# Token parts of 256 and 288 instead of 272 and 272 in the projections, and a 64 byte tile beside h

## The chip, the core and the metric

The kernel runs on one core of one Trainium2 chip. The metric is device time in microseconds (us) for one launch; lower is better. TensorE is PE in the profile, its weight loads are PEld, VectorE is DVE, ScalarE is ACT, GpSimd is POOL, SyncE is SP, and SP issues the DMA transfers.

## What is computed

One inference step of a one-layer decoder. There are 512 prompt tokens and 32 sample tokens (8 requests of 4), 544 in all, of width 1024. The reference, cut to what the change touches:

```python
shift, scale, gate = split(silu(c) @ w_cond + b_cond, 3)
h = x * (1 + scale[:, None]) + shift[:, None]
[qa, ka, va, za, qkv_b, zb, a_b, b_b, g_a, g_b] = h @ w_in      # 1024 -> 11280
ya = o_a * silu(za)                       # o_a: dilated attention, three head groups
yb = rms_norm(o_b) * silu(zb)             # o_b: gated delta rule after a short convolution
merged = sigmoid(g_a) * (ya @ w_branch_a) + sigmoid(g_b) * (yb @ w_branch_b)
y = layer_norm(ALPHA * x + gate[:, None] * (merged @ w_out)) * ln_g + ln_b
```

It also returns the new key and value caches, convolution states and delta-rule states.

## The kernel before

**Projections.** Features lie on the partitions, tokens along the free dimension. A weight of 128 output columns arrives as a tile `wt` of 128 x 1024 float32 (8 blocks of 128 x 128, one for each 128 input features). `split` makes of it `hi` (ACT, rounded to float32r) and `lo` (DVE, the rest). The activations are kept in the same two pieces, `hhi` and `hlo` (h), `ybh` and `ybl` (branch B), `yah` and `yal` (branch A), `x1h` and `x1l` (the first tiles). Each 128 x 128 block needs three products: `hi` with the high part of h, `hi` with its low part, `lo` with the high part. In the profile these stand as `pp<-hhi,hi`, `pp<-hlo,hi` and `pp<-hhi,lo`: output, moving operand, weights. All are float32r.

**Two parts.** One PSUM tile (`pp`, 2 buffers) holds at most 512 float32 in a partition, so the 544 tokens are taken in two parts of `HF` = 272. `stream` runs a job's 24 products (8 blocks x 3) for part 0, hands the sum to the job's `evac`, and does the same for part 1. Each product loads its weights anew. There are 85 tiles of `w_in` in this loop, 8 of `w_branch_b`, and 8 of `w_branch_a` with 4 blocks instead of 8. The first three tiles of `w_in` are done ahead of it, from `x1h` and `x1l` with sums in `pp`, `pd` and `pg`. The `evac` functions (`conv_job`, `attention_job`, `za_job`, `zb_job`, `gate_job`, `branch_job`) know where a part ends: the prompt's last 240 tokens and the 32 sample tokens are in part 1.

**The last stage.** `product_out` multiplies `mhi` and `mlo` (weights) with `wo0h`, `wo0l` (first 512 output columns) and `wo1h`, `wo1l` (the other 512) in products of 512 columns, and in two products of 256 for the last 128 tokens. It doesn't use `HF`.

**Addresses.** The pools `wsp` (two buffers each of `hi` and `lo`) and `hpool` (`hhi`, `hlo`) are allocated one after the other from the right end of SBUF, and the pool of `ybh` and `yal` behind them. One token row of h takes 544 x 4 = 2176 = 17 x 128 bytes, a part of 272 takes 1088 = 8 x 128 + 64. In the built program `hi` and `lo` begin at 96 modulo 128 in every buffer and block. `hhi` and `hlo` also begin at 96, so part 0 begins 0 bytes from the weights modulo 128, part 1 begins 64 bytes from them (`ybh` and `yal` likewise; `x1h`, `x1l`, `ybl` and `yah` begin at 32, so that it is the other way round there). `mhi` and `mlo` lie at 32 modulo 128, `wo0h` and `wo0l` at 32 (0 bytes apart), `wo1h` at 96 (64 bytes apart).

**Order.** The program is first recorded, then put in order by a list scheduler (`schedule`) that keeps a cost for each instruction (a float32r product's grows with its columns) and emits the instructions in its order of start, so that each engine's queue is fixed at build time. Attention, the delta rule and the sample tokens' work are put between the projection's products. SP issues all transfers in that order: weights, cache rows for the sample tokens, and the copies of old cache rows to the outputs (`out_kv_s<-in_cache`), which are spread over the span. All engine instructions are emitted by one line of `emit`, L727, so rows are told apart by tile names.

Of the kernel before, what the change touches and what calls it, by code (L numbers as in the profile page):

```python
# [23 lines left out]
NTD = 4  # L24
NS = NB * NTD
NT = SEQ + NS
HF = NT // 2
PROJ = 11280
OFF_Q, OFF_K, OFF_V, OFF_ZA, OFF_B, OFF_ZB, OFF_AB, OFF_GA, OFF_GB = (
    0, 1536, 3072, 4608, 5120, 8192, 9216, 9232, 10256)  # L30
# [219 lines left out]
class Recorder:  # L250
# [21 lines left out]
    def pool(self, make, name, bufs, side):  # L272
        return Pool(self, make, name, bufs, side)
# [506 lines left out]
def body(ctx, tc, io):  # L780
# [11 lines left out]
    keep = pool(ctx, "keep", 1)  # L792
    wsp = pool(ctx, "wsp", 2, "right")
    hctx = ExitStack()
    hpool = pool(hctx, "hpool", 1, "right")
    psp = bank("psp", BANKS[0])
    psd = bank("psd", BANKS[1])
# [13 lines left out]
    def pp():  # L811
        return psp.tile([128, 512], F32, name="pp", tag="pp")
# [79 lines left out]
    abT = op.tile([128, NT], F32, name="abT", tag="o")[0:32]  # L892
    xs = xT[:, :, SEQ:].rearrange("p k (b t) -> p k b t", t=4)
    per_token = lambda t, k, n: t[:, k:k + n, 1:9, None].to_broadcast([128, n, 8, 4])
    cols_of = lambda n: slice(n * HF, (n + 1) * HF)
    with ExitStack() as fctx:
        fr = pool(fctx, "front", 1)
        cT = fr.tile([128, KT, 9], F32, name="cT")
# [59 lines left out]
            return pv[:, :, 0:9], bT[:, 8 * part + at:8 * part + at + m, None].to_broadcast([128, m, 9])  # L958

        x1 = [fr.tile([128, KT, NT], F32R, name=f"x1{u}") for u in "hl"]  # L960
        sums = [[f()[:, :HF] for _ in range(2)] for f in (pp, pd, pg)]
        for b, (c, m) in enumerate(CHUNKS):
            pv, bias = cond_block(1, c, m, b % 2)
            kk = slice(c, c + m)
# [26 lines left out]
        for n in range(2):  # L991
            for k in range(KT):
                for x in range(2):
                    pe.matmul(ps[n][0:32, :HF], hl[:, k], x1[x][:, k, cols_of(n)],
                              start=(k == 0 and x == 0), stop=(k == KT - 1 and x == 1))
        for n in range(2):
            se.activation(abT[:, cols_of(n)], ps[n][0:32, :HF], AF.Copy)
        for c, m in two_by_two:
            pv, bias = cond_block(0, c, m, c % 4)
            kk = slice(c, c + m)  # L1000
# [42 lines left out]
    def stream(until):  # L1043

        while done[0] < until:
            i = done[0]
            job = jobs[i]
            for x in range(i, min(i + 5, len(jobs))):
                if x not in raws:
                    raws[x] = wraw.tile([128, D], F32, name="wt", tag="wraw")  # L1050
                    jobs[x].load(raws[x])
                if x <= i + 1 and x not in weights:
                    weights[x] = split(raws[x], jobs[x].nk * 128, ve)
            if job.start:
                yield job.start
            if job.begin:
                job.begin()
            (hi, lo), (xhi, xlo) = weights.pop(i), job.x
            for n in range(2):
                ps = pp()[:, :HF]  # L1060
                cols = slice(n * HF, (n + 1) * HF)
                for k in range(job.nk):
                    a, b = hi[:, k * 128:(k + 1) * 128], lo[:, k * 128:(k + 1) * 128]
                    for w, x in ((a, xhi), (a, xlo), (b, xhi)):
                        pe.matmul(ps, w, x(k)[:, cols], start=(k == 0 and w is a and x is xhi),
                                  stop=(k == job.nk - 1 and w is b))
                    if k < job.nk - 1:
                        yield 0
                job.evac(n, ps)
                if n and job.after:  # L1070
                    job.after()
                if not n:
                    yield 0
            done[0] += 1
            threads.set(job.over, 0.0)
            yield 0
# [4 lines left out]
    def column_job(name, **kw):  # L1081
        return Job(name[0], lambda raw: sp.dma_start(raw, io["w_in"][TILE_AT[name]]), KT, of_h, **kw)

    half = lambda t, n: t[:, n * HF:(n + 1) * HF]


    moves = [(g, b, r, min(r + MOVE, w - 4)) for g, (w, _) in enumerate(GROUPS) for b in range(8) for r in range(0, w - 4, MOVE)]
# [133 lines left out]
    def conv_job(h, s):  # L1221
# [19 lines left out]
        def evac(n, ps):  # L1241
            if not n:
                head_of_ext()
                se.activation(t["ext"][:, 3:275], ps, AF.Copy)
                return
            ext = t["ext"]
            es = ext[:, 515:571].rearrange("p (b w) -> p b w", w=7)
            se.activation(ext[:, 275:515], ps[:, 0:240], AF.Copy)
            se.activation(es[:, :, 3:7], ps[:, 240:272].rearrange("p (b t) -> p b t", t=4), AF.Copy)
            convolve()  # L1250

        def shifted(raw, by):
# [290 lines left out]
    def attention_job(j, g, s):  # L1543

        def begin():
            pairs[j][s, g] = spare()[:, :SEQ] if s == 2 else ap.tile([128, 512], F32, name="qk"[s], bufs=3)

        def evac(n, ps):
            t, scale = pairs[j][s, g], 1.0 if s else -0.125
            if g == 0:  # L1550
                lo, hi = ((0, 272), (272, 512))[n]
                se.activation(t[:, lo:hi], ps[:, 0:hi - lo], AF.Copy, scale=scale)
            else:
                v = t.rearrange("p (r a n) -> p n a r", r=4, a=4)
                m = (17, 15)[n]
                se.activation(v[:, 17 * n:17 * n + m], ps[:, 0:16 * m].rearrange("p (n a r) -> p n a r", a=4, r=4),
                              AF.Copy, scale=scale)
            if n:
                se.activation((qs, ks, vs)[s][:, j, g if s else at_g(g), :], ps[:, 240:272], AF.Copy, scale=scale)
                if s == 2:  # L1560
                    threads.set(ready[j, g], 2.5)

        return column_job(("a", j, g, s), evac=evac, begin=begin, start=(freed[j - 1] if j else began,))
# [954 lines left out]
```

## Time and profile before

| | |
|---|---|
| median of 3 runs | 886.1 us (883.63 to 886.37) |
| profiled execution, span | 886.1 us |
| TensorE clock granted, mean | 0.995 |
| PE | 864.7 us, 8176 instructions |
| DVE, ACT, POOL | 643.4, 451.7, 68.7 us |
| DMA | 236.18 MB, queue q1 79.0% of 16 engines' span |

[...] Products overlap, so the time that one costs in a run of products is the distance from one start to the next, here called the interval. It is read from the timeline's starts or from a long run in the chain of waits, divided by the count.

### The profile page before, as it was taken

Reading aid. Unit: us, or ns where it says so; the run is one execution under the profiler, and the core shown is the slowest. Engines: PE = TensorE matmul, PEld = TensorE weight load, DVE = VectorE, ACT = ScalarE, POOL = GpSimd, SP = SyncE. Lnnn points to the kernel's source line nnn. Section 1 sums busy time; section 2 is a strip of 40 time slices with the busy share of each in tenths; the row PEclk is TensorE's granted clock in tenths of the full one; section 3 lists DMA queues with packets and bytes.
Section 4 is the critical chain, followed back from the end, with each engine's and each line's share of the span. In section 5 each row is a group of like instructions: output and inputs, shape, how many; then the busy total and the mean of one; then the engine's idle time right before and its main releaser. Section 6 shows DMA issues by size and latency. Waiting matters only on the chain.

```text
span 886.1 us, 20733 instructions
## 1 busy us (share of the span) xinstructions
PE 864.7 (98%) x8176; PEld 818.1 (92%) x8176; DVE 643.4 (73%) x1330; ACT 451.7 (51%) x1073; POOL 68.7 (8%) x167
## 2 busy tenths in 40 slices
PE   8999999999999999999999999999999999999994
PEld 7889999898999899999999988999899999999884
DVE  4675557564458899968999753556899699998547
ACT  3546656765546696347775446732442222324324
POOL 0120110110001110002120000021010000001000
PEclk9999999999999999999999999999999999999998
DMA  9876768666687886889877885479869899987973
GB/s 334 337 212 199 234 219 268 235 206 214 198 256 249 282 278 207 271 265 329 303 227 257 262 291 186 169 219 293 330 223 375 275 402 420 377 285 235 348 248 142
DMA packets 121069, 236.18 MB, mean 267 GB/s; under 512 B 49174, under 2 KB 76640, under 8 KB 118284
## 3 DMA queue, kind: packets, MB, share of 16 engines
q1 hardware_dynamic: 120972, 234.86, 79.0%
q8 instruction: 64, 1.05, 0.5%
q14 instruction: 33, 0.27, 0.1%
HBM read 218.53 MB, written 103.97 MB: 364 GB/s over the span
## 4 chain that ended last, share of the span: by engine, by line
PE 82%; DMA 6%; DVE 5%; ACT 5%; issue 1%; SPq 1%; POOL 0%; DVEq 0%; ACTq 0%
PE pp L727 62%; PE pg L727 9%; PE pd L727 7%; PE pb L727 4%; DMA wc<-in_w_cb 2%; ACT L727 1%; DVE r L727 1%; DMA slab<-in_ks 1%; DMA dO<-orow 1%; DMA S<-in_state_delta 1%; DMA wv<-dw 1%; ACT hi L727 1%; DMA out_kv_s<-in_cache 1%; SPq L727 1%; ACT sq L727 1%
## 5 line engine op out<-in xcount | busy, mean ns | idle before, releaser
L727 PE MATMUL pp<-hhi,hi 128*128 128x272 f32 x1360 | 400.2, 294 | 1.7 <-DVE zt L727 1.0
L727 PE MATMUL pp<-hhi,lo 128*128 128x272 f32 x1360 | 401.3, 295 | 0.0
L727 PE MATMUL pp<-hlo,hi 128*128 128x272 f32 x1360 | 398.1, 293 | 0.0
L727 PEld LDWEIGHTS pp<-hhi,hi 128*128 128x128 f32 x1360 | 257.0, 189 | 4.6 <-issue 1.8
L727 PEld LDWEIGHTS pp<-hhi,lo 128*128 128x128 f32 x1360 | 256.7, 189 | 2.1 <-issue 1.4
L727 PEld LDWEIGHTS pp<-hlo,hi 128*128 128x128 f32 x1360 | 257.1, 189 | 1.5 <-issue 0.4
L727 ACT ACTIVATE hi<-wt 128x1024 fp32r<-128x1024 f32 (+1 forms) x101 | 103.6, 1026 | 171.2 <-PE pp L727 130.1
L727 DVE TENSOR_TENSOR lo<-wt,hi 128x1024 fp32r<-128x1024 f32 (+1 forms) x101 | 119.0, 1178 | 74.9 <-ACT hi L727 74.4
L727 DVE SCALAR_TENSOR_TENSOR acc<-ext,cw,acc 128x568 f32<-128x568 f32 x72 | 58.0, 805 | 1.6 <-ACT acc L727 0.6
L727 DVE TENSOR_TENSOR slab<-slab 128x512 f32<-128x512 f32 (+1 forms) x66 | 43.1, 669 | 6.7 <-DMA slab<-in_ks 4.5
L727 DVE TENSOR_REDUCE slab<-slab 128x8 f32<-128x512 f32 (+2 forms) x66 | 42.7, 660 | 3.3 <-ACT slab L727 3.0
L727 ACT ACT_TABLE_LOAD x32 | 41.1, 1283 | 4.1 <-DMA dO<-orow 1.6
L727 ACT ACTIVATE zt<-pp 128x272 f32<-128x272 f32 x48 | 18.7, 390 | 38.7 <-PE pp L727 37.3
L727 PE MATMUL pp<-ybh,lo 128*128 128x272 f32 x128 | 36.9, 288 | 0.0
L727 PE MATMUL pp<-ybh,hi 128*128 128x272 f32 x128 | 36.9, 288 | 0.0
L727 PE MATMUL pp<-ybl,hi 128*128 128x272 f32 x128 | 36.9, 288 | 0.0
L727 ACT ACTIVATE P<-P,st 128x256 f32<-128x256 f32 (+1 forms) x64 | 31.1, 488 | 11.2 <-DVE st L727 11.1
L727 POOL COPY cx<-ext 128x3 f32<-128x3 f32 (+1 forms) x48 | 21.7, 480 | 151.0 <-ACT ext L727 149.5
L727 DVE CUSTOM_DVE_ANT_0 P<-pg,bias 128x256 f32<-128x256 f32 (+1 forms) x64 | 23.0, 403 | 13.8 <-PE pg L727 13.7
L727 ACT ACTIVATE spare<-pp 128x272 f32<-128x272 f32 (+1 forms) x32 | 16.2, 506 | 16.1 <-PE pp L727 16.1
L727 PEld LDWEIGHTS pp<-ybh,hi 128*128 128x128 f32 x128 | 24.1, 189 | 0.2
L727 PEld LDWEIGHTS pp<-ybh,lo 128*128 128x128 f32 x128 | 24.2, 189 | 0.1
(421 smaller groups left out, 1548.8 us busy)
## 6 DMA issues: line engine op xcount, KB each, us to landing
out_kv_s<-in_cache SPq DMA_DIRECT2D x144, 512.0 KB
wt<-in_w_in SPq DMA_DIRECT2D x85, 512.0 KB
out_kv_s<-in_cache SPq DMA_DIRECT2D x24, 496.0 KB
wc<-in_w_cb SPq DMA_DIRECT2D x16, 512.0 KB
slab<-in_ks SPq DMA_DIRECT2D x32, 256.0 KB
slab<-in_vs SPq DMA_DIRECT2D x32, 256.0 KB
kv<-in_ks SPq DMA_DIRECT2D x16, 512.0 KB
kv<-in_vs SPq DMA_DIRECT2D x16, 512.0 KB
```

Source lines behind the costliest of these rows:

```text
L727: getattr(real[x.engine], x.name)(*map(arg, x.args), **{k: arg(v) for k, v in x.kw.items()})
```

## The change

Every projection takes its tokens as 256 and 288 instead of 272 and 272: `HF` goes, `HALVES` and `WIDTH` come, and each `evac` uses the new bounds (256 prompt tokens in part 0; 256 prompt and 32 sample tokens in part 1). A pool `apart` with one tile `gap` of 16 float32 (64 bytes) is opened between `wsp` and `hpool`, and GpSimd clears it once. In the built program `hi` and `lo` stay at 96 modulo 128, and `hhi`, `hlo`, `ybh` and `yal` are at 32; `x1h`, `x1l`, `ybl` and `yah` stay at 32. 256 columns take 1024 = 8 x 128 bytes, so both parts now begin 64 bytes from the weights modulo 128.

```diff
-HF = NT // 2
+HALVES = (slice(0, 256), slice(256, NT))
+WIDTH = (256, NT - 256)
...
     hctx = ExitStack()
+    apart = pool(hctx, "apart", 1, "right")
+    gap = apart.tile([128, 16], F32, name="gap")
+    ge.memset(gap, 0.0)
     hpool = pool(hctx, "hpool", 1, "right")
...
-    cols_of = lambda n: slice(n * HF, (n + 1) * HF)
+    cols_of = lambda n: HALVES[n]
...
-        sums = [[f()[:, :HF] for _ in range(2)] for f in (pp, pd, pg)]
+        sums = [[f()[:, :w] for w in WIDTH] for f in (pp, pd, pg)]
...
             for n in range(2):
-                ps = pp()[:, :HF]
-                cols = slice(n * HF, (n + 1) * HF)
+                ps, cols = pp()[:, :WIDTH[n]], HALVES[n]
...
-                se.activation(t["ext"][:, 3:275], ps, AF.Copy)
+                se.activation(t["ext"][:, 3:259], ps, AF.Copy)
...
-            se.activation(ext[:, 275:515], ps[:, 0:240], AF.Copy)
-            se.activation(es[:, :, 3:7], ps[:, 240:272].rearrange("p (b t) -> p b t", t=4), AF.Copy)
+            se.activation(ext[:, 259:515], ps[:, 0:256], AF.Copy)
+            se.activation(es[:, :, 3:7], ps[:, 256:288].rearrange("p (b t) -> p b t", t=4), AF.Copy)
...
-                m = (17, 15)[n]
-                se.activation(v[:, 17 * n:17 * n + m], ps[:, 0:16 * m].rearrange("p (n a r) -> p n a r", a=4, r=4),
+                se.activation(v[:, 16 * n:16 * n + 16], ps[:, 0:256].rearrange("p (n a r) -> p n a r", a=4, r=4),
                               AF.Copy, scale=scale)
```

The scheduler's costs change with the columns, so a few instructions change places. On PE, in the first tiles of attention, the transposes of the value tile (`pg<-cst,spare`) and of a delta-rule head (`pb<-cst,KQ`) stand between a projection's products. Before:

```order
L727 MATMUL pp<-hlo,hi 128x272
L727 MATMUL pp<-hhi,lo 128x272
L727 MATMUL pg<-cst,spare 128x128 x2
L727 MATMUL pp<-hhi,hi 128x272
L727 MATMUL pp<-hlo,hi 128x272
L727 MATMUL pp<-hhi,lo 128x272
L727 MATMUL pp<-hhi,hi 128x272
L727 MATMUL pp<-hlo,hi 128x272
L727 MATMUL pb<-cst,KQ 128x128 x4
L727 MATMUL pp<-hhi,lo 128x272
```

Now, on the same engine at the same place:

```order
L728 MATMUL pp<-hhi,lo 128x288
L728 MATMUL pp<-hhi,hi 128x288
L728 MATMUL pg<-cst,spare 128x128 x2
L728 MATMUL pp<-hlo,hi 128x288
L728 MATMUL pp<-hhi,lo 128x288
L728 MATMUL pp<-hhi,hi 128x288
L728 MATMUL pp<-hlo,hi 128x288
L728 MATMUL pp<-hhi,lo 128x288
L728 MATMUL pb<-cst,KQ 128x128 x4
L728 MATMUL pp<-hhi,hi 128x288
```

Five products stand between the two groups as before; each group stands one product further on. Of the 4800 float32r projection products with 128 output features, 4535 were followed directly by another before, and 4528 are now.

On SP, in the middle of the program, the cached keys of the sample tokens (`slab`), a weight tile (`wt`) and the copies of cache rows are issued in turn. Before:

```order
L727 DMA slab<-in_ks 128x512
L727 DMA wt<-in_w_in 128x1024
L727 DMA slab<-in_ks 128x512
L727 DMA out_kv_s<-in_cache 16x8192
L727 DMA slab<-in_ks 128x512 x2
L727 DMA out_kv_s<-in_cache 16x8192
L727 DMA slab<-in_ks 128x512 x2
```

Now, on SP at the same place:

```order
L728 DMA slab<-in_ks 128x512 x2
L728 DMA wt<-in_w_in 128x1024
L728 DMA out_kv_s<-in_cache 16x8192
L728 DMA slab<-in_ks 128x512 x2
L728 DMA out_kv_s<-in_cache 16x8192
L728 DMA slab<-in_ks 128x512 x2
```

One more piece of the cached keys now stands ahead of the weight tile; the copies keep their places between the others.

More of the change, by code (lines that the diff above doesn't have):

```diff
@@ L993, in body @@
                 for x in range(2):
-                    pe.matmul(ps[n][0:32, :HF], hl[:, k], x1[x][:, k, cols_of(n)],
+                    pe.matmul(ps[n][0:32, :WIDTH[n]], hl[:, k], x1[x][:, k, cols_of(n)],
                               start=(k == 0 and x == 0), stop=(k == KT - 1 and x == 1))
         for n in range(2):
-            se.activation(abT[:, cols_of(n)], ps[n][0:32, :HF], AF.Copy)
+            se.activation(abT[:, cols_of(n)], ps[n][0:32, :WIDTH[n]], AF.Copy)
         for c, m in two_by_two:
@@ L1082, in column_job @@
         return Job(name[0], lambda raw: sp.dma_start(raw, io["w_in"][TILE_AT[name]]), KT, of_h, **kw)
-    half = lambda t, n: t[:, n * HF:(n + 1) * HF]
+    half = lambda t, n: t[:, HALVES[n]]
     moves = [(g, b, r, min(r + MOVE, w - 4)) for g, (w, _) in enumerate(GROUPS) for b in range(8) for r in range(0, w - 4, MOVE)]
@@ L1550, in evac @@
             if g == 0:
-                lo, hi = ((0, 272), (272, 512))[n]
-                se.activation(t[:, lo:hi], ps[:, 0:hi - lo], AF.Copy, scale=scale)
+                se.activation(t[:, 256 * n:256 * n + 256], ps[:, 0:256], AF.Copy, scale=scale)
             else:
                 v = t.rearrange("p (r a n) -> p n a r", r=4, a=4)
-                m = (17, 15)[n]
-                se.activation(v[:, 17 * n:17 * n + m], ps[:, 0:16 * m].rearrange("p (n a r) -> p n a r", a=4, r=4),
+                se.activation(v[:, 16 * n:16 * n + 16], ps[:, 0:256].rearrange("p (n a r) -> p n a r", a=4, r=4),
                               AF.Copy, scale=scale)
             if n:
-                se.activation((qs, ks, vs)[s][:, j, g if s else at_g(g), :], ps[:, 240:272], AF.Copy, scale=scale)
+                se.activation((qs, ks, vs)[s][:, j, g if s else at_g(g), :], ps[:, 256:288], AF.Copy, scale=scale)
                 if s == 2:
```

## The prediction

> **What bounds the kernel now.** I read the page first, then the chain of waits, then the stages, then single intervals in the timeline of TensorE.
>
> ```profile
> span 886.1 us, 20733 instructions
> PE 864.7 (98%) x8176; PEld 818.1 (92%) x8176; DVE 643.4 (73%) x1330; ACT 451.7 (51%) x1073; POOL 68.7 (8%) x167
> ...
> PE 82%; DMA 6%; DVE 5%; ACT 5%; issue 1%; SPq 1%; POOL 0%; DVEq 0%; ACTq 0%
> ...
> L727 PE MATMUL pp<-hhi,hi 128*128 128x272 f32 x1360 | 400.2, 294 | 1.7 <-DVE zt L727 1.0
> L727 PE MATMUL pp<-hhi,lo 128*128 128x272 f32 x1360 | 401.3, 295 | 0.0
> L727 PE MATMUL pp<-hlo,hi 128*128 128x272 f32 x1360 | 398.1, 293 | 0.0
> ```
>
> The profiled span equals the median of the runs, 886.1 us, so the sum below is made against it with nothing added. TensorE is occupied for 98% and its largest group waits 1.7 us in all. Its stream of products sets the end; what one product costs in that stream is the question. The 294 ns of the page is not that cost, since products overlap. The chain gives it in long unbroken runs (start, length, count):
>
> ```profile
> 375.18 18.12 PE pp L727 x144
> 690.73 47.05 PE pp L727 x374
> ```
>
> 18.12/144 = 125.8 ns and 47.05/374 = 125.8 ns for one product of 272 columns. The granted clock is 1.00 in the windows below, so no throttle explains the number. Now the two parts apart. In h's job, 24 products make a part; the rows are first products of three parts in turn, the first part with its operands 64 bytes apart modulo 128 (tokens 272 to 543), the next 0 bytes apart:
>
> ```profile
> 376.28 0.29 PE L727 MATMUL pp<-hhi,hi 128*128 128x272 f32 x1
> ...
> 379.28 0.29 PE L727 MATMUL pp<-hhi,hi 128*128 128x272 f32 x1
> ...
> 382.32 0.29 PE L727 MATMUL pp<-hhi,hi 128*128 128x272 f32 x1
> ```
>
> 3.00/24 = 125.0 ns at 64 bytes, 3.04/24 = 126.7 ns at 0 bytes. **The distance alone is worth under 2 ns at 272 columns.** The last stage holds the other cases: `wo0h` lies 0 bytes from its weights, `wo1h` 64. The products of 256 columns, first and last row of 30 and of 48, and between them products of 512 at 64 bytes:
>
> ```profile
> 844.82 0.28 PE L727 MATMUL pp<-wo0h,mhi 128*128 128x256 f32 x1
> ...
> 848.27 0.28 PE L727 MATMUL pp<-wo0h,mlo 128*128 128x256 f32 x1
> ...
> 866.79 0.40 PE L727 MATMUL pp<-wo1l,mhi 128*128 128x512 f32 x1
> ...
> 869.35 0.28 PE L727 MATMUL pp<-wo1h,mhi 128*128 128x256 f32 x1
> ...
> 874.68 0.28 PE L727 MATMUL pp<-wo1h,mlo 128*128 128x256 f32 x1
> ```
>
> 256 columns at 0 bytes: 3.45/29 = 119.0 ns. 256 at 64 bytes: 5.33/47 = 113.4 ns. 512 at 64 bytes: 2.56/11 = 232.7 ns. Is the 113.4 only a quieter machine? The windows of these two stretches, and of the three parts of 272 above, say no (columns: length, then PE, PEld, DVE, ACT, POOL busy with counts, clock, DMA share, GB/s):
>
> ```profile
> 869.35:874.68 5.33, 5.33 (x48) 5.32 (x47) 5.14 (x11) 3.57 (x7) 0.00 (x0) 1.00 0.26 98
> 844.82:848.27 3.45, 3.45 (x31) 3.45 (x30) 0.42 (x1) 0.04 (x1) 0.00 (x0) 1.00 0.57 179
> 376.28:388.36 12.08, 12.08 (x99) 12.08 (x97) 10.80 (x31) 4.49 (x8) 0.00 (x0) 1.00 0.87 249
> ```
>
> The fast stretch is the one in which VectorE is full and ScalarE at two thirds; in the slow one both are nearly idle. The DMA was busier in the slow one, 0.57 against 0.26, but the run of 374 products kept its 125.8 ns beside a DMA share of 1.01 (the window from 700 us, below) as the other did at 0.87. I take it that address distance and length together set the interval.
>
> **The change part by part.** Products: 3 x 1360 of h, 3 x 128 of `ybh` and `ybl`, 3 x 64 of `yah` and `yal`, 9 groups of 16 of the first tiles: 4080 + 384 + 192 + 144 = 4800, in 2400 pairs of parts. Rows for the smaller groups:
>
> ```profile
> L727 PE MATMUL pp<-ybh,hi 128*128 128x272 f32 x128 | 36.9, 288 | 0.0
> ...
> L727 PE MATMUL pp<-yah,hi 128*128 128x272 f32 x64 | 18.5, 291 | 0.2 <-ACT yah L727 0.2
> ...
> L727 PE MATMUL pp<-x1l,hi 128*128 128x272 f32 x16 | 4.9, 313 | 0.0
> ```
>
> A pair costs 125.0 + 126.7 = 251.7 ns now. None is removed and none added; 16 columns move from one part to the other.
>
> *The part of 256.* Its nearest row has the same columns and the same distance: 113.4 ns. Bounds: 113.4 and 119.0 (the row at 0 bytes). I take 113.4, since in that stretch the interval was steady from the first product behind one of 512, and the weights there (`mhi`, `mlo`) came from 16 different tiles, so that no more than the distance modulo 128 was held fixed.
>
> *The part of 288.* No row shows 288. From below, 113.4 x 288/256 = 127.6 ns, if it runs at the good rate. From above, 126.7 x 288/272 = 134.2 ns. Two rows at the right distance, 64 bytes, stand on either side: 272 columns gave 125.0, which scales to 132.4; and on the line from 272 (125.0) to 512 (232.7), 16 columns more give 132.2. Both sides of 288 were slow at 64 bytes, although 512 columns, like 288, are a whole number of 128 bytes. So I take 132.3 ns: the second part gets nothing but its columns.
>
> *Sum.* 113.4 + 132.3 = 245.7 ns, 6.0 ns less for a pair. By the order of TensorE, 4535 of the 4800 products are followed directly by another; where a product of another kind stands behind, the columns cancel between the parts and I count nothing. 2267 pairs x 6.0 ns = 13.6 us.
>
> *What may not follow.* Two stages run near another limit:
>
> ```profile
> 340.00:380.00 40.00, 39.79 (x312) 39.07 (x311) 36.01 (x83) 19.65 (x50) 0.25 (x2) 1.00 0.78 245
> ...
> 700.00:760.00 60.00, 60.00 (x529) 59.07 (x529) 53.57 (x59) 16.61 (x29) 0.00 (x0) 1.00 1.01 402
> ```
>
> VectorE at 90% still has room for a TensorE that is 2.4% faster. The DMA engines are full from 700 to 760 us; if they hold the weights back there, 60 x 6.0/251.7 = 1.4 us is not gained. I count half, 0.7 us. In the order of SP one piece of the cached keys now stands ahead of a weight tile:
>
> ```profile
> slab<-in_ks SPq DMA_DIRECT2D x32, 256.0 KB
> ...
> L727 POOL COPY cx<-ext 128x3 f32<-128x3 f32 (+1 forms) x48 | 21.7, 480 | 151.0 <-ACT ext L727 149.5
> ```
>
> 256 KB at the 245 GB/s of the window from 340 us is some 1 us, hidden by the weight tiles loaded ahead: there are three `wt` buffers, each worth 24 x 251.7 ns = 6.0 us of products.
>
> *The small edits.* ScalarE's copies out of PSUM have the same total of columns. GpSimd's clear of `gap` is one small instruction at the start, on an engine that is busy 8%; if it were not covered it would cost some 0.5 us, as the copy of three columns does (480 ns, the row above). The first part is shorter, so its PSUM buffer must be emptied within 132.3 x 24 = 3.2 us instead of 3.0, the second within 2.7; the groups wait 1.7 us in all now, and I count nothing.
>
> 886.1 - 13.6 + 0.7 = 873.2, rounded to **873 us**.
>
> [...]
>
> **The rivals.** About 0.3% (2.7 us) is what a measurement here can tell from no change.
>
> 1. *Both parts run at the good rate.* For it: both are whole multiples of 128 bytes long and 64 apart, as in the steady stretch. Against it: 512 columns at 64 bytes, also a whole multiple, took 232.7, above 2 x 113.4 = 226.8. Pair 113.4 + 127.6 = 241.0: 10.7 x 2267 = 24.3 us, 862 us.
>
> 2. *The distance does nothing in the loop; only columns count.* For it: under 2 ns at 272. In the loop the moving tiles step by 2176 bytes and not by 2048 as `wo1h` does, and products of another kind come between. Pair 119.0 + 132.3 = 251.3: 0.4 x 2267 = 0.9 us, 885 us. The case that the change doesn't do what it says, since a distance fixed at build time makes no steady pattern in the loop, is this one.
>
> 3. *The part of 288 locks to the bad side: slower.* A steady pattern can be steadily bad. In a run of 272 some intervals are longer:
>
> ```profile
> 375.76 0.30 PE L727 MATMUL pp<-hhi,lo 128*128 128x272 f32 x1
> 375.90 0.29 PE L727 MATMUL pp<-hhi,hi 128*128 128x272 f32 x1
> 376.03 0.28 PE L727 MATMUL pp<-hlo,hi 128*128 128x272 f32 x1
> ```
>
> 0.27/2 = 135 ns. If every product of the second part were like that, plus 16 columns at 125.8/272 = 0.46 ns, it would be 142.4 ns, the pair 255.8, and 4.1 x 2267 = 9.3 us are lost: 895 us. It decides from 251.7 - 113.4 = 138.3 ns on. Against it: at 64 bytes both longer lengths have means near the others.
>
> **How the numbers follow.** The chances: forecast 0.50, both good 0.20, nothing 0.17, slower 0.13. The forecast's own range: 288 columns between 512's rate (232.7 x 288/512 = 130.9 ns) and that of the mixed runs (125.8 x 288/272 = 133.2), so 7.4 to 5.1 ns for a pair, 16.8 to 11.6 us, with 0 to 1.4 us lost to the DMA and 2 us either way for waits that change place: 868 to 878 us. The range for 8 in 10 reaches to both neighbours, 860 to 888 us. Faster by over 0.3%: the first two cases less a little for lost waits, 0.68; within 0.3%: 0.18, nearly all of it rival 2; slower: 0.14.
>
> **What would show it.** The rows of `128x256` and `128x288` in the profile after, and their intervals in long runs: 113.4 and 132.3 ns are forecast; 127.6 for the second is rival 1, 119 for the first rival 2, above 138.3 for the second rival 3. TensorE's waits should stay within a few us, and the rows of the last stage should keep their intervals. The forecast is wrong if the first part isn't steady at 113 in the loop, or if the stage from 700 to 760 us keeps its length.

## The result and the profile after

The median went from 884.32 us (882.89 to 886.53, 7 runs) to **890.22 us** (887.29 to 893.27, 7 runs). The ratio is 1.0057 with a 95% interval of 1.0035 to 1.0080: slower, by about 5 us. The forecast was 873, and the range of 860 to 888 does not hold it. (Further down, one run of `e10_order_268`, 940.54 us at a granted clock of 0.848, is left out of its median and ratio.) The profiled execution has a span of 888.5 us, against 886.1 before. The page after, in the rows that answer to those shown of before (span, engines, shares of the chain of waits, largest group):

```profile
span 888.5 us, 20739 instructions
PE 862.7 (97%) x8176; PEld 815.7 (92%) x8176; DVE 643.3 (72%) x1329; ACT 454.6 (51%) x1076; POOL 62.9 (7%) x168
...
PE 86%; DMA 5%; DVE 5%; ACT 2%; issue 1%; SPq 0%; DVEq 0%; ACTq 0%
...
L728 PE MATMUL pp<-hhi,hi 128*128 128x256 f32 (+1 forms) x1360 | 400.1, 294 | 1.5 <-DVE spare L728 1.0
```

TensorE is busy 2.0 us less in a span that is 2.4 us longer. So its products did get a little cheaper, and time in which it does nothing came in. First the products: the timeline of TensorE after, the first products of four parts in turn, 24 products to a part (first the start, then the duration):

```profile
374.88 0.29 PE L728 MATMUL pp<-hhi,hi 128*128 128x288 f32 x1
...
378.05 0.28 PE L728 MATMUL pp<-hhi,hi 128*128 128x256 f32 x1
...
380.86 0.29 PE L728 MATMUL pp<-hhi,hi 128*128 128x288 f32 x1
...
384.03 0.28 PE L728 MATMUL pp<-hhi,hi 128*128 128x256 f32 x1
```

3.17/24 = 132.1 ns for 288 columns, as forecast; 2.81/24 = **117.1 ns** for 256, where 113.4 was forecast. Over the loop (all products that directly follow another, intervals under 180 ns) the means are 132.1 and 117.4, the pair 249.5. The same means before were 125.9 and 125.2, the pair 251.1. So 1.6 ns of a pair were gained, not 6.0: 1.6 x 2267 = 3.6 us. A long unbroken run in the chain of waits after agrees (start, length, count):

```profile
687.03 52.66 PE pp L728 x422
```

52.66/422 = 124.8 ns, half of 249.5, in the stage in which the DMA engines are full (DMA share 0.97 from 700 to 760 us in after, 1.01 before); before it was 125.8 there.

Now the loss. The list of TensorE's waits (total, times, longest) begins with one that the kernel before doesn't have:

```profile
PE pg L728 <- DVE o L728: 2.9, 1, 2.9
```

It is the end of the sample tokens' late attention: VectorE reduces the last scores (`od`), makes `om` and `o`, and TensorE transposes `o`. The windows around it (length, PE, PEld, DVE, ACT, POOL, clock, DMA share, GB/s):

```profile
793.70:796.50 2.80, 0.01 (x2) 0.00 (x0) 2.53 (x5) 0.00 (x0) 0.00 (x0) 1.00 0.90 338
796.00:798.00 2.00, 1.42 (x7) 1.45 (x8) 1.11 (x6) 0.39 (x4) 0.00 (x0) 0.68 1.08 373
798.00:800.00 2.00, 2.00 (x10) 2.00 (x10) 0.78 (x5) 0.19 (x2) 0.00 (x0) 0.50 0.47 180
800.00:802.00 2.00, 2.00 (x16) 2.00 (x16) 0.56 (x3) 0.63 (x1) 0.00 (x0) 0.97 0.00 0
```

TensorE stands for 2.8 us, and then runs for about 3.4 us at a lowered clock, granted at 0.50 from 797 to 800 us. At that clock a product of 256 columns took 0.214 us (three of them start at 797.36, 797.58 and 797.79 us), so the slow stretch cost some 1.7 us more. With the slow stretch behind it this one wait comes to 2.9 + 1.7 = 4.6 us: the gain of the products and 1 us beyond it. The timed runs show the lower clock too: its mean was 0.990 to 0.994 in the seven runs of after, and 0.995 or more in ten of the twelve runs of `e1_before_order` below; 3.41 us at half the clock take 0.0019 off that mean.

### The profile page after: what moved, and what is told of

It reads as the page before. It is cut to its first block, busy times and chain, and to the rows that moved or that the text cites. A ratio compares the mean times of both kernels' runs of the same rounds, so it can differ in the third digit from the quotient of the medians.

```text
span 888.5 us, 20739 instructions
## 1 busy us (share of the span) xinstructions
PE 862.7 (97%) x8176; PEld 815.7 (92%) x8176; DVE 643.3 (72%) x1329; ACT 454.6 (51%) x1076; POOL 62.9 (7%) x168
## 4 chain that ended last, share of the span: by engine, by line
PE 86%; DMA 5%; DVE 5%; ACT 2%; issue 1%; SPq 0%; DVEq 0%; ACTq 0%
PE pp L728 65%; PE pg L728 9%; PE pd L728 8%; PE pb L728 4%; DMA wc<-in_w_cb 2%; DVE r L728 1%; DMA slab<-in_ks 1%; DMA wt<-in_w_in 1%; DVE lo L728 1%; DMA rbo<-dO 1%; ACT hi L728 1%; DMA wt<-in_w_ga 1%; ACT L728 0%; DVE od L728 0%; DMA out_kv_p<-spare 0%
## 5 line engine op out<-in xcount | busy, mean ns | idle before, releaser
L728 PE MATMUL pp<-hhi,hi 128*128 128x256 f32 (+1 forms) x1360 | 400.1, 294 | 1.5 <-DVE spare L728 1.0
L728 PE MATMUL pp<-hlo,hi 128*128 128x256 f32 (+1 forms) x1360 | 398.1, 293 | 0.0
L728 PE MATMUL pp<-hhi,lo 128*128 128x256 f32 (+1 forms) x1360 | 397.1, 292 | 0.0
L728 ACT ACTIVATE zt<-pp 128x256 f32<-128x256 f32 (+1 forms) x48 | 18.7, 390 | 38.5 <-PE pp L728 34.3
L728 PE MATMUL pp<-ybl,hi 128*128 128x288 f32 (+1 forms) x128 | 37.1, 290 | 0.0
L728 PE MATMUL pp<-ybh,lo 128*128 128x288 f32 (+1 forms) x128 | 36.9, 289 | 0.0
L728 PE MATMUL pp<-ybh,hi 128*128 128x288 f32 (+1 forms) x128 | 36.9, 288 | 0.0
L728 DVE SCALAR_TENSOR_TENSOR zt<-zt,pp 128x256 f32<-128x256 f32 (+1 forms) x32 | 13.7, 432 | 15.1 <-PE pp L728 9.0
```

Of the source, the lines that this page charges most:

```text
L728: getattr(real[x.engine], x.name)(*map(arg, x.args), **{k: arg(v) for k, v in x.kw.items()})
```

## The experiments

Two questions stand apart: is the loss from the products' addresses or from the new order, and why did 256 columns not run at 113.4 ns.

**1. The change in the order of before, and the order of after without the change.** The planner works out its costs from column counts. In `e1_before_order` it reckons both parts as 272 columns wide, which gives the order of before on every engine but for the one clear of `gap`; the instructions stay those of the change. `e2_after_order` is the reverse: the kernel before, its parts of 272 reckoned as 256 and 288, which gives the order of after. `e3_gap_alone` is the kernel before with the tile.

```diff
-        size = lambda v: math.prod(v.shape[1:])
+        size = lambda v: self.seen.get(math.prod(v.shape[1:]), math.prod(v.shape[1:]))
...
+    seen = ({256: 272}, {288: 272, 256: 240})       # e1; e2: ({272: 256}, {272: 288, 240: 256})
...
+                    rec.seen = seen[n]               # around the products and evac of part n
```

> Parts of 256 and 288 and the 64 byte tile as in the change, but every engine has the order of before: the planner still reckons both parts as 272 columns. Theory A (the products give 3.6 us, and the new order takes back more than that): 3 to 5 us faster than before, about 881 us against 884; the first kv load behind sbb goes out ahead of the weight load again, and TensorE's wait at 792 to 797 us is gone. Rival B (the new lengths and addresses themselves cost the time): as slow as the changed kernel, about 890 us. In both, the part of 256 takes 117 to 118 ns and the part of 288 132 ns in the loop, as in the changed kernel's trace.

> The kernel before with both parts of 272 and without the tile, but in the order of the changed kernel: the planner reckons the parts as 256 and 288. Theory A: 6 to 10 us slower than before, 890 to 894 us, with the weight load ahead of the seven kv loads behind sbb and a wait of TensorE of some 4 us near 790 us. Rival B: within 2 us of before, 884.

> The kernel before with the 64 byte tile alone: parts of 272, the order of before. The first part now lies 64 bytes from its weights and the second 0, where it was the other way round. Theory A: the two swap places and a pair still costs 251.7 ns; within 1.5 us of before. Rival B (the moved addresses of h cost something of their own): 3 us slower or more.

| kernel | time, us | ratio to before | profiled span |
|---|---|---|---|
| change, order of before (e1) | 885.27 | 1.0013 (0.9993 to 1.0033) | 883.0 |
| before, order of after (e2) | 892.96 | 1.0082 (1.0056 to 1.0108) | 891.7 |
| before and the tile (e3) | 886.58 | 1.0018 (1.0002 to 1.0035) | 884.1 |

The order alone makes the kernel before slower by 0.8%, more than the change does; the change without the order loses nothing. So **the loss is the order's**. The order differs in much more than the few places shown ahead of the prediction: by the rows of the traces before and after, at least 951 of TensorE's 8176 instructions, 278 of VectorE's 1330, 196 of ScalarE's 1073 and 119 of SP's 767 would have to be moved to turn one into the other, and one `vn` went from VectorE to ScalarE. e2 has the same new wait, with products that are all of 272 columns (list of waits of e2):

```profile
PE pg L727 <- DVE o L727: 2.8, 1, 2.8
```

The same product in two kernels tells where it goes. Two rows of TensorE's timeline after, the 4529th and the 4649th of the 4800 products of the projections:

```profile
786.64 0.28 PE L728 MATMUL pp<-hlo,hi 128*128 128x256 f32 x1
...
808.12 0.29 PE L728 MATMUL pp<-yal,hi 128*128 128x288 f32 x1
```

And the same two products in e1:

```profile
785.44 0.28 PE L728 MATMUL pp<-hlo,hi 128*128 128x256 f32 x1
...
802.85 0.29 PE L728 MATMUL pp<-yal,hi 128*128 128x288 f32 x1
```

After lies 1.2 us behind e1 at the first and 5.3 us at the second; at the last product it is 5.8. So 4.1 of 5.8 us arise in these 20 us, around the wait. e2 against before gives the same picture: 1.3, 5.3 and 5.9 us.

What in the order is worse there, VectorE's timeline shows. After:

```profile
705.77 1.23 DVE L728 TENSOR_TENSOR lo<-wt,hi 128x1024 fp32r<-128x1024 f32 x1 [4.17 <-ACT hi L728]
...
707.97 1.22 DVE L728 TENSOR_TENSOR kv<-kv,qr 128x1024 f32<-128x1024 f32 x1
...
745.18 0.53 DVE L728 CUSTOM_DVE_ANT_0 Sa<-pg,sba 128x352 f32<-128x352 f32 x1 [1.43 <-PE pg L728]
...
791.52 0.69 DVE L728 TENSOR_TENSOR lo<-wt,hi 128x512 fp32r<-128x512 f32 x1
...
793.59 1.21 DVE L728 TENSOR_REDUCE od<-kv 128x8 f32<-128x1024 f32 x1
...
796.14 0.29 DVE L728 TENSOR_TENSOR o<-om 128x128 f32<-128x128 f32 x1
```

In e1:

```profile
701.59 1.23 DVE L728 TENSOR_TENSOR kv<-kv,qr 128x1024 f32<-128x1024 f32 x1 [1.81 <-DMA kv<-in_ks]
704.55 1.23 DVE L728 TENSOR_TENSOR lo<-wt,hi 128x1024 fp32r<-128x1024 f32 x1 [1.74 <-ACT hi L728]
...
739.24 0.52 DVE L728 CUSTOM_DVE_ANT_0 Sa<-pg,sba 128x352 f32<-128x352 f32 x1 [1.24 <-PE pg L728]
...
787.90 1.22 DVE L728 TENSOR_REDUCE od<-kv 128x8 f32<-128x1024 f32 x1
...
790.46 0.29 DVE L728 TENSOR_TENSOR o<-om 128x128 f32<-128x128 f32 x1
...
791.96 0.69 DVE L728 TENSOR_TENSOR lo<-wt,hi 128x512 fp32r<-128x512 f32 x1
```

In e1 the attention's tail (the last `od`, `om`, `o`) is over before the split `lo` of the next weight tile; after, that split stands ahead of the last two `od`. The tail is late long before this: `Sa`, a step of the same attention some 50 us earlier, already lies 5.9 us behind e1. Counted in VectorE's rows, 86 of the 101 splits stand ahead of `Sa` and 94 ahead of `o` in after; in e1 85 and 93. So the chain stands one split later in the queue. A split can't run ahead of TensorE: it needs `hi`, of which there are two buffers, and ScalarE writes the next one when the products let it (timeline of ScalarE after):

```profile
704.68 1.06 ACT L728 ACTIVATE hi<-wt 128x1024 fp32r<-128x1024 f32 x1 [2.27 <-PE pp L728]
...
710.67 1.06 ACT L728 ACTIVATE hi<-wt 128x1024 fp32r<-128x1024 f32 x1 [4.33 <-PE pp L728]
```

From one `hi` to the next are 6.0 us, the time of a tile's 48 products (24 x 249.5 ns), and one split more ahead of the tail makes it later by about that: 5.9 us at `Sa`, 5.7 at `o`. (For the last two `hi` ahead of `o` in after, 784.83 and 790.86 us, the profile names the weights' transfer; they too are 6.0 us apart.) At the end VectorE's own work holds the tail as much: from 747 us to `o` it is idle for 0.38 us in all, 0.10 of it ahead of the split at 791.52.

The tail then ends at 796.4 us and not at 790.8. In e1 TensorE has 16 projection products between the attention's last output (`pg<-kv,PTa`) and the transpose of `o`; in after it has none left there, and waits.

**2. Can the tail be brought forward by one edit?** `e5_kv_ahead` is after with one weight load on SP put behind three loads of the tail's `kv`, since the first late step that I saw was a late `kv` load. `e6_kv_early` adds that VectorE takes the three `kv` products ahead of the split that waits 4.17 us for `hi`. `e7_less_vector` is after, and leaves out three of the sixteen `kv` by `Sb` products of the late attention, to take 3.5 us of work off VectorE; the rest is as it was.

```diff
+        self.order.remove(loads[at])                  # e5: the weight load behind the third kv load
+        self.order.insert(self.order.index(loads[at + 3]) + 1, loads[at])
...
+            self.order.insert(self.order.index(low), x)   # e6, besides: each of three kv products ahead of lo
...
+        for x in late[11:14]:                         # e7, alone: three kv * Sb products left out
+            self.order.remove(x)
```

> The changed kernel with one edit in SP's order: the weight load that stands between sbb and the seven kv loads is moved behind the third of them, where the kernel before has it. Theory A with this place as its whole cause: the late sample attention ends 3 to 4 us earlier, TensorE's 4 us at 790 to 806 us come back, and the kernel is 3 to 4 us faster than the changed one, about 886 us. Rival C (the order costs at several places, this one is only where the trace shows it): less than 1.5 us faster than the changed kernel, 889 to 890.

> The changed kernel with two edits in its order near 700 us: in SP's order the weight load between sbb and the seven kv loads goes behind the third of them (as in the run before), and in VectorE's order the first three products on those loads go ahead of the weight split in front of which VectorE waits 4.2 us. Theory A2 (the late sample attention is a chain on VectorE; it slipped there, its end holds TensorE at 793.7 to 796.6 us for 2.9 us, and the halved clock behind that wait costs 1.6 us more): the chain ends 2 to 3.4 us earlier, the wait falls below 1 us, the clock stays at 1.00 there, and the kernel is 3 to 4.5 us faster than the changed one, 886 to 887 us. Rival C (the loss is spread over the order): less than 1.5 us faster.

> The changed kernel without three of the sixteen products of kv and Sb in the late sample attention (1.13 us each on VectorE), so that part of that attention is left out; all orders as in the changed kernel. Theory A3 (in the new order this chain on VectorE ends last: it holds TensorE for 2.9 us, and the halved clock behind that wait costs 1.6 us): with the chain some 3 us shorter the wait at 793 us nearly goes, the clock stays at 1.00 there, and the kernel is 3.5 to 5 us faster than the changed one, 885.5 to 887 us. Rival C (the loss lies elsewhere): less than 1.5 us faster, 889 to 890.

| kernel | time, us | ratio to before |
|---|---|---|
| e5 | 891.27 | 1.0062 (1.0037 to 1.0086) |
| e6 | 893.00 | 1.0086 (1.0061 to 1.0111) |
| e7 | 891.48 | 1.0065 (1.0039 to 1.0091) |

None gave the loss back. In e6 the products did run early, and it was lost again at the next split (VectorE's timeline of e6):

```profile
705.94 2.49 DVE L740 TENSOR_TENSOR kv<-kv,qr 128x1024 f32<-128x1024 f32 x2 [0.20 <-DMA kv<-in_ks]
...
719.84 1.23 DVE L740 TENSOR_TENSOR lo<-wt,hi 128x1024 fp32r<-128x1024 f32 x1 [2.52 <-ACT hi L740]
```

After has that split at 717.76. The products of e6 lie 2.08 us behind those of after from 664 us on, ahead of the first place that the edit touches, so the split is no earlier than in after. In e7 the same happens at the end, though VectorE has less to do. Its timeline in e7:

```profile
786.95 0.69 DVE L734 TENSOR_TENSOR lo<-wt,hi 128x512 fp32r<-128x512 f32 x1 [2.60 <-ACT hi L734]
```

And the list of TensorE's waits in e7:

```profile
PE pg L734 <- DVE o L734: 2.9, 1, 2.9
```

VectorE waits 2.6 us for `hi`, which itself waits for TensorE's products (786.28 us on ScalarE, 2.13 us `<-PE pp`), and the tail is as late as before: `o` starts at 797.60 us, 1.46 us behind after, and the products of e7 lie 1.45 us behind those of after as well. So neither the late `kv` load nor VectorE's load of work is the cause by itself. What the three share is that 94 splits still stand ahead of `o`, as in after, and that a split waits for TensorE. That this one place in the queue is the cause fits all three; no run moved the tail by that one split and nothing else, so it is argued and not shown (the table at the end of part 4 bears on it).

**3. The interval of a product, by itself.** Behind the end of the kernel before, TensorE runs series of 48 products with nothing else on the core, built like those of the loop (8 blocks of 3, each with its own weights), but with operands that are all zero. Varied are the columns, the bytes from one block's moving operand to the next (the step), and the distance of the operands (`phase` is the shift, in 4 byte words). The times of these launches contain the series and are not compared.

```diff
+    for c, (n, phase, step, ws, lo, turns) in enumerate(CASES):
+            for k in range(8):
+                w0, w1 = (W[:, 1024 * u + ws * k:1024 * u + ws * k + 128] for u in (0, 1))
+                x0, x1 = (X[:, phase + lo * u + step * k:phase + lo * u + step * k + n] for u in (0, 1))
+                for j, (w, x) in enumerate(((w0, x0), (w0, x1), (w1, x0))):
+                    nc.tensor.matmul(ps[:, :n], w, x, start=(k == 0 and j == 0), stop=(k == 7 and j == 2))
```

> The kernel before, and behind its end 49 series of 48 products (96 in the first) with nothing else at work: weights from a tile at step 512 bytes, two tiles (hi, lo) in the loop's order, lengths 256, 272, 288 and 512, moving rows at steps of 2048, 2176 and 2304 bytes, and a distance between the operands of 0, 32, 64, 96, 128 and 192 bytes. Theory P (distance modulo 128 and length alone set the interval, as the prediction took it): 256 at 64 bytes takes 113.4 ns at every step, 288 takes 132, 272 takes 125 to 127. Theory Q (the step of the moving rows counts too: it is 2048 bytes where 113.4 was seen and 2176 in the loop): 256 at 64 bytes takes 113.4 at 2048 and 117 to 118 at 2176. Theory R (the good rate comes from what other engines do): none of the series shows 113.4, or all of 256 do.

Rows of the chain of waits, 24 products each. At the loop's step of 2176 bytes, 256, 272 and 288 columns at 64 bytes; then 256 at a step of 2048 bytes, at 192 bytes:

```profile
911.96 2.80 PE pg L2492 x24
...
946.62 3.01 PE pc L2492 x24
...
983.54 3.17 PE pg L2492 x24
...
1037.51 2.73 PE pa L2492 x24
```

2.80/24 = 116.7 ns is the best that 256 columns reach at the loop's step; 272 and 288 give 125.4 and 132.1. **On a quiet core the loop's products are no faster than in the loop.** The last row, 2.73/24 = 113.7, is the good rate: in this series it comes only at the step of 2048 bytes, and of the six distances tried there only 192 bytes has it (the others 117.9 to 119.9). So theory P fails, and Q with it, since 64 bytes don't give the rate at 2048 either.

> The kernel before, and behind its end 45 more series of 48 products with nothing else at work. In the first set of series one case of 256 columns ran at 113.6 ns, with rows at steps of 2048 bytes and the operands 192 bytes apart; all others of 256 took 116.6 to 119.9. Theory S (what counts is that the distance stays the same modulo 256, and that it is 192): 256 at a distance of 192 takes 113 to 114 ns also at a step of 2304 bytes, and, for the two products in three that read the high part, at a step of 4352 bytes with high and low rows alternating, 115 to 117 as a mean there. Rival T (the case at 2048 was a pattern of its own): 117 to 120 everywhere, at 192 too. 288 columns: 131.5 to 133.5 at every distance by both.

> The kernel before, and behind its end 29 more quiet series of 48 products. One case of 256 columns ran at 113.6 ns twice (rows at steps of 2048 bytes, 192 bytes from the weights). Here high and low rows lie interleaved at that step (the low part 1024 bytes behind the high one), both operands are shifted together, and the low rows are shifted against the high ones. Theory V (the good rate needs the step of 2048 and the 192 bytes between the operands, nothing else): 113 to 114 ns interleaved and with both shifted by 32, 64 or 128 bytes, lost where the low rows are shifted. Rival W (a chance pattern of that one layout): 116 to 120 in all of them but the repeated one. 32, 64 and 128 columns: no expectation.

From the chain of waits of the second series, 256 columns at 192 bytes, at a step of 2304 and then of 2048 bytes:

```profile
1008.38 2.83 PE pg L2488 x24
...
1056.72 2.73 PE pg L2488 x24
```

From that of the third, the same at 2048 bytes with the high and low parts of the moving operand interleaved 1024 bytes apart, and then with both operands shifted by 128 bytes:

```profile
922.48 2.72 PE pb L2472 x24
...
936.34 2.83 PE pg L2472 x24
```

The good rate of 113.3 to 114.0 came at steps of 1024, 2048, 3072 and 4096 bytes with the operands 192 bytes apart modulo 256; 16 bytes off it was lost (119.2), and it was lost too when both operands moved by 64 or 128 bytes (117.8), though not by 32, and at a step of 2304 bytes (117.7), where the distance stays the same modulo 256. So the distance isn't all of it (theory S fails, V in part), and 64 modulo 128, the change's idea and mine, is neither sufficient nor the right modulus. At 288 columns no step or distance gave anything but 131.1 to 133.5; 272 columns, 124.6 to 126.7 elsewhere, took 123.4 at a step of 2048 and 192 bytes.

`e4_no_tile` asks the same of the kernel: parts of 256 and 288 without the tile, in the order of before.

```diff
-    apart = pool(hctx, "apart", 1, "right")
-    gap = apart.tile([128, 16], F32, name="gap")
-    ge.memset(gap, 0.0)
```

> Parts of 256 and 288 without the 64 byte tile, in the order of before: both operands lie 0 bytes apart modulo 128. Theory U (an interval is 0.46 ns for each column, whatever the address; the quiet series gave 118.8 for 256 columns at distance 0 and 116.6 at 64, 133.3 and 132.2 for 288): the parts take 118 to 119 and 132 to 133.5 ns in the loop, 251 to 252 for a pair as before; within 0.3% of before and of the kernel with the tile in this order (885.3 us). Rival (the tile is what the change lives on): 3 us or more slower than that one.

It took 886.48 us, 1.0008 (0.9991 to 1.0024). Its intervals are 118.4 and 133.0 ns, against 117.4 and 132.2 with the tile (e1). By the intervals the tile is worth 1.0 + 0.8 = 1.8 ns on a pair, 4.1 us; the two ratios show nothing of it.

**4. A version with the good rate.** `e9_rows_2048` keeps the order of before and puts the first parts of `hhi` and `hlo` into one tile, so that a row takes 2048 bytes; a second small tile brings the distance to 192 modulo 256. Each of the 16 writes of h becomes two.

```diff
+    both.extend(t.pool.real.tile([128, KT, 2, w], t.dtype, name=n) for n, w in (("h0", WIDTH[0]), ("h1", WIDTH[1])))
...
+    edge = pool(ctx, "edge", 1, "right").tile([128, 16], F32, name="edge")
+    ge.memset(edge, 0.0)
     wsp = pool(ctx, "wsp", 2, "right")
```

> Parts of 256 and 288 in the order of before, and h stored anew: the first parts of high and low rows lie together, so that a row is 2048 bytes, 192 bytes from the weights modulo 256, with the weights at 160 modulo 256 (64 bytes are laid aside ahead of them), the layout in which the quiet series of 256 took 113.8 ns; the second parts follow apart. Each of the sixteen writes of h is made in two. Theory V (addresses alone set the interval): 256 columns take 113 to 114 ns in the loop now, 288 132 to 133, a pair 246 against 249.5 of the changed kernel and 251.1 before; on TensorE that is 11 us less than before in sum, of which between a third (as much as the run with the order of before showed) and all arrives: 874 to 882 us. Rival X (in the loop the other engines' reads and writes break the pattern): 116 to 118 ns as in the changed kernel, 884 to 886 us.

885.29 us, 0.9996 (0.9980 to 1.0012): the good rate is there in part, the time is not. TensorE's timeline of e9, the first products of three parts:

```profile
376.57 0.40 PE L761 MATMUL pp<-h,hi 128*128 128x256 f32 x2
...
379.32 0.42 PE L761 MATMUL pp<-h,hi 128*128 128x288 f32 x2
...
382.49 0.40 PE L761 MATMUL pp<-h,hi 128*128 128x256 f32 x2
```

2.75/24 = 114.6 ns and 3.17/24 = 132.1. Over the loop the mean of h's 256 columns is 115.7 ns, against 117.4 in e1, and in stretches of 20 us it lies between 114.1 and 117.7: between V and X. Between 700 and 740 us it is 117.4. The chain of waits of e9 has there:

```profile
685.88 47.25 PE pp L761 x374
```

and that of e1, for the same 374 products in the same order:

```profile
688.11 47.07 PE pp L728 x374
```

And the window of e9 of the same time (columns as above):

```profile
700.00:760.00 60.00, 60.00 (x532) 59.07 (x531) 56.53 (x62) 15.92 (x27) 0.00 (x0) 1.00 1.01 405
```

47.25/374 = 126.3 ns, no better than 125.9 in e1 and 125.8 before. The DMA engines are full there, but they are not shown to be the reason: from 740 to 760 us, at a DMA share of 1.00, the 256 columns take 115.6 ns again. The profile of e9 ends 2.3 us before e1's (880.7 against 883.0); the timed runs don't confirm even that.

Since the order counts for more than the products, three more orders of the same kernel were tried, each from a slightly different reckoning of the widths:

```diff
-    seen = ({256: 272}, {288: 272, 256: 240})
+    seen = ({256: 268}, {288: 276, 256: 244})       # and 271 / 273, 278 / 266
```

> The kernel with rows of 2048 bytes (885.3 us in the order of before), in another order: the planner reckons the two parts as 268 and 276 columns, 4 away from before. The instructions and their addresses are the same in this run and the next two, only places in the queues differ. Theory D (the order is a draw: any small change of the reckoned costs gives another plan, whose waits fall out by chance, and the change's 5.8 us were such a draw): the three orders differ from the order of before and from one another by several us, with no relation to how far the numbers were moved; this one between 0 and 10 us slower. Rival E (the order follows the costs smoothly, and 256 and 288 are simply far from 272): 268 within 1.5 us of the order of before.

> As the run before, with parts reckoned as 271 and 273 columns. Theory D: another order again, between 3 us faster and 10 us slower than 885.3. Rival E: within 1 us of 885.3.

> As the two runs before, with parts reckoned as 278 and 266 columns, further from before than 268. Theory D: between 3 us faster and 10 us slower than 885.3, and not bound to be worse than 268. Rival E: worse than 271, and as far from before as 268 or further.

| reckoned widths | time, us | ratio to the runs of before taken with it |
|---|---|---|
| 272 / 272 (e9) | 885.29 | 0.9996 (0.9980 to 1.0012) |
| 271 / 273 | 884.38 | 1.0001 (0.9978 to 1.0025) |
| 268 / 276 | 888.32 | 1.0039 (1.0022 to 1.0056) |
| 278 / 266 | 886.31 | 1.0020 (1.0001 to 1.0038) |

Four columns in the planner's head are worth 0.4%: 268 lies 3.0 us from the order of before, where E allows 1.5. 271 is within 1 us, as E has it, and 278 is 1.0 us off, with an interval that reaches into that of 268; several us between all of them, as D has it, were not seen. None of these orders beats the kernel before, and no version that was run does so measurably.

`e10_order_268` has the wait again, 4.3 us for `o` at the same place. By the splits that stand ahead of `Sa` and `o` on VectorE, the traces of all thirteen kernels (without the three series) fall into two groups:

| splits ahead of `Sa`, `o` | kernels | TensorE's wait for `o` | profiled spans | median times |
|---|---|---|---|---|
| 85, 93 | before, e1, e3, e4, e9, e10 with 271 and 278 | at most 0.15 us | 878.9 to 886.3 | 884.3 to 886.6 |
| 86, 94 | after, e2, e5, e6, e7, e10 with 268 | 2.8 to 4.3 us | 886.9 to 892.1 | 888.3 to 893.0 |

So in every kernel that was run the loss goes with the tail's one split, whatever the products are.

## Why the prediction was wrong

*The part of 288* was right: 132.3 forecast, 132.1 measured, on a line that the quiet series continue from 240 columns (112.3 ns) to 304 (139.6).

*The part of 256* is **the first step that failed**. It took 113.4 ns from the last stage's `wo1h`, and got 117.1. The reason given there was that the weights came from 16 tiles, "so that no more than the distance modulo 128 was held fixed". The step was held fixed as well: `wo1h` moves by 2048 bytes from block to block and h by 2176, and in the quiet series the good rate came at steps of 1024, 2048, 3072 and 4096 bytes, and not at 2176, 2304 or 4352. Rival 2 names that very difference in one clause, as a point in its favour, and I gave it 0.17. The upper bound, 119.0, held: the value lay 2/3 of the way to it. With the measured pair the term is 1.6 x 2267 = 3.6 us instead of 13.6.

*What may not follow* is **the second, and it decided the sign**. It allowed 2 us either way "for waits that change place". The exchange of places cost 5.8 us between two profiles of the same products (after and e1), and by e2's ratio 0.82% of 886 us, 7 us. I had compared the orders on TensorE and SP, and quoted places that look harmless; the loss shows on VectorE, where one more split, paced by TensorE, had come ahead of the late attention, so that its tail was 5.7 us late and TensorE waited for it. The wait's own length is not the price either: 2.9 us of it were followed by 1.7 us more at a granted clock of 0.50, where a product of 256 columns took 0.214 us.

*The stage from 700 to 760 us*: 0.7 us were set aside. With the small gain that came the stage kept pace (124.8 ns for a product, as in the rest), and TensorE is busy for all of its 60 us in after as in e9, so no run shows the term. What e9 lost there it lost in the interval of 256 columns, for a reason that stays open.

*The small edits* at nothing: the tile alone gave 1.0018 (1.0002 to 1.0035), which just excludes none. Its intervals, 125.9 and 125.4 ns, are those of before, so no mechanism for a loss is seen.

*Rival 1* (both at the good rate, 862 us) fell with 288 columns, which have no good rate at any address tried. *Rival 3* (288 locked to the bad side) fell too. *Rival 2* forecast 119.0 and 132.3 for the products and 885 us; the products are 117.4 and 132.1, and the change in the order of before took 885.27. It was the nearest account of the products. That the kernel came out slower and not equal is the order, for which no case stood in the list: the slower case that stood there was put on the products.

What e1 leaves open: by 3.6 us from the products it should be measurably faster than before, and 1.0013 (0.9993 to 1.0033) shows no gain. Its profiled span is 1.1 us below e3's; product by product it is 0.2 us behind e3 at the 2001st of the 4800 (370 us) and 1.1 us ahead at the last, so the first 370 us kept nothing of the gain. Why is not shown. The runs of one kernel scatter over 7 us (e1: 882.05 to 889.78, the two longest at the lowest clocks, 0.992 and 0.993), so a gain of 2 us is at the edge of what could be seen.

## What to carry to other kernels

A steady rate seen in one stage came here with all of that stage's addresses, the step from operand to operand among them (256 columns took 113.4 ns at `wo1h`'s step of 2048 bytes and 117.1 at h's of 2176); before it is carried over, it is to be measured in a quiet series with the addresses of the place it is wanted for. Where a planner's costs depend on the sizes that are changed, the change is two changes: the same instructions in the old order, and the old instructions in the new order, tell them apart, and here the second was the larger. When orders are compared, the place to look is each in-order queue: count how many instructions that are paced by the bottleneck (here the splits) stand ahead of the end of a chain that the bottleneck itself will wait for. One more was worth about 6 us of lateness here.

## What the runs showed of the hardware that was not expected

- **From 240 to 512 columns a product's cost was nearly all columns.** With its own weights, from 240 to 304 columns, the quiet series gave 240: 111.9 to 112.6, 256: 116.6 to 119.9, 272: 124.6 to 126.7, 288: 131.1 to 133.5, 304: 139.0 to 140.1 ns: about 0.43 ns for each further column, by the means at both ends (139.6 - 112.3)/64, on some 10 ns that don't depend on them. 512 columns took 227.7 to 231.2, which lies on that line. Addresses moved it by 1 or 2%, and only 256 columns had a distinctly better rate, 113.3 to 114.0 ns (272 had 123.4 once).
- **A wait of 2.9 us was followed by half the clock** for 3.4 us; e1 and e3, without such a wait, have no window of low clock ahead of their last stage. In the thirteen traces all eight waits of TensorE of 2.7 us or more ahead of the last stage (2.7 to 4.3 us) came with such a window; behind those for `o` in after, e2, e5, e6 and e7 the lowest clock in windows of 2 or 4 us was 0.50 to 0.57. Shorter ones came with one or not. One that did is in after: a row of TensorE's timeline with its wait in brackets,

```profile
543.15 0.37 PE L728 MATMUL pg<-k,q 64*128 64x128 f32 x1 [1.99 <-issue]
```

and the window behind it, TensorE full at a clock of 0.57:

```profile
544.00:548.00 4.00, 4.00 (x65) 3.70 (x65) 3.15 (x9) 3.09 (x8) 0.67 (x1) 0.57 0.03 8
```

So did 1.51 us before (ending at 520.70 us, a clock of 0.64 from there to 524 us) and 1.46 us in e4 (522.20); 1.57 us in after (422.25, a clock of 1.00 from there to 427 us), 2.02 in e5 (423.58, 1.00 over 400 to 500 us) and 2.51 in `e10_order_278` (416.68) did not. So below 2.7 us the length of the wait doesn't decide it alone. Small products stood around these waits, and no run varied one of the two alone.
- **Short products lost the clock without any wait.** In the third series products of 32 columns took 2.59/24 = 108 ns at a granted clock of 1.00, back to back; a few us later they, and those of up to 128 columns, took 5.12/24 = 213 ns at a granted clock of 0.50, with TensorE busy throughout. Two rows of the third series' chain of waits:

```profile
1022.55 2.59 PE pe L2472 x24
...
1028.71 5.12 PE pg L2472 x24
```

And its window behind them (columns as above):

```profile
1030.00:1080.00 50.00, 50.00 (x235) 50.00 (x236) 0.00 (x0) 0.00 (x0) 0.00 (x0) 0.50 0.00 1
```

32 columns at a clock of 1.00 are not on the line of 240 to 304 columns, by which 10 + 0.43 x 32 = 24 ns would be expected. At 0.50 products of 32, 64 and 128 columns all took 213 ns, and in after those of 256 took 0.214 us. So there the interval didn't follow the columns; what sets it no run shows.
